# The fourth token sum of a seven-product FFN, issued in pieces among the first chain's products

## The chip, the cores and the metric

The kernel runs on one core of one Trainium2 chip. The metric is the device time of one execution in microseconds (us). The core has TensorE (PE in the profile; PEld is its loading of weights), VectorE (DVE), ScalarE (ACT), GpSimd (POOL) and SyncE (SP); the last two issue most of the DMAs here.

## What is computed

Two layers of a decoder on 512 tokens of width 1024. The first layer mixes tokens with dilated attention, the second with a recurrent block, and each is followed by a gated convolutional FFN, which is what the change touches:

```python
def conv_ffn(x, w_up, conv_w, conv_b, w_down):
    u = causal_dwconv(x @ w_up, conv_w, conv_b)      # (512, 6144), three taps along the tokens
    g, v = u[..., :D_FF], u[..., D_FF:]              # D_FF = 3072
    return (jax.nn.gelu(g, approximate=True) * v) @ w_down
```

All data are float32. Norms stand before and after each part.

## The kernel before, in words

**Precision.** A float32 operand is split (`split`, L148) into a rounded half `hi` (ScalarE, L149) and the residue `lo` (VectorE, L150). A product is three passes, hi x hi, hi x lo and lo x hi. Weights come as blocks of 1 MB by SyncE (`load`, L331), at most three at a time, and are split on the way.

**The up projection.** Its output is made in tiles of 128 features by 512 tokens; twelve groups j of 256 features for g and twelve for v. Groups 0 to 2 are made plainly (`feat_tile`, L623: one weight, all tokens, 24 matmuls of 512 columns). Groups 3 to 11 (`SEVEN`, L39) are made by a scheme of Strassen's kind (`seven`, L1047): a 256 x 512 x 1024 product is cut into two by two blocks and made from seven block products instead of eight, at the price of sums. Nine groups times two halves (g, v) are the 18 chains. A chain (L1010) has seven products of twelve matmuls of 256 columns, numbered 1 to 7. Their left operands are blocks of a raw weight or sums of them, made in place: s1, w11, w12, s2, s3, s4, a22. VectorE makes some of these sums (L210, L214), and GpSimd the others, as DMAs that add (L186). Their right operands are blocks of the activations hT, or one of four sums T of them, made once per FFN by `token_sums` (L918).

**Slots.** `seven` gives every product a slot number m (`AT`, L41): in a chain that starts at 10 n, product 1 stands at 10 n, 5 at +1, 2 at +2, 6 at +4, 3 at +5, 7 at +8, 4 at +13. So the products of the first chain stand at m = 0, 1, 2, 4, 5, 8 and 13, those of the second from m = 10 on. Free slots (m = 9, 16, 17, 19 and so on) take quarters of a plain tile or early parts of the down projection. Numbers with nothing in them are passed over. In each slot (`slot`, L365) the product is issued first, then what earlier slots put off (`later`, L362), then a `tick` (L377). What is put off are copies of part results (`part`, ScalarE, L1032), sums of part results (L1036, L1041), and the tile's end: eviction with the first tap (ScalarE, L773), two more taps (VectorE, L777), gelu (ScalarE, L795) or gate (VectorE, L799). Product 6 accumulates into the bank of product 1, so it has to wait for the copy of product 1's result; product 3 likewise for product 5's.

**Ticks.** A tick advances the generators in `sides` (each yields the number of ticks to its next step), then calls `pump` (L303) unless `state["hold"]` is set:

```python
        if not state["hold"]:
            pump(1 if state["even"] or state["live"] >= HALVES - 4 else 2)
```

`pump` takes the next piece of weight from a fixed order (`stream`, L199), splits it into one of 16 pairs of buffers, issues the sums that stand behind it in the order, and loads the next raw block when the last piece of an old one is taken. `live` counts the buffers in use; a product frees its own (`done`, L354). While `seven` runs, `state["even"]` is set: one piece per tick. If a product's piece has not been split when the product is issued, `take` (L347) pumps it then.

**The token sums.** `token_sums` runs as such a generator beside the plain tiles. With first=False (the FFN) it starts at the FFN's fifth tick and takes one tick per step: keep x and take buffers; add the two halves of hT's blocks back together (L939); T0 = b11 - b12 and its split; b22; two more differences (L964, L945); the split of T1; the split of T2; then, at the twelfth tick, b21 and its two differences (L945); at the thirteenth the split of the last sum, T3 (two tiles, homes 6 and 7). `seven` starts after the fourteenth. T3 is the right operand of product 4, which the first chain has at m = 13. Attention calls the same function with first=True and two ticks to a step.

The engines take their instructions in the order of issue, each from its own queue, so the order in which slots and ticks issue them sets what stands in front of what.

Of the kernel before, what the change touches and what calls it, by code (L numbers as in the profile page):

```python
# [32 lines left out]
HALVES = 16  # L33
# [8 lines left out]
CYCLE = 10  # L42
# [41 lines left out]
def kernel(  # L84
# [38 lines left out]
    def nm(s):  # L123
        uid[0] += 1
        return f"{s}{uid[0]}"

    def gen(dt=F32, s="g"):
        return gp.tile([P, 512], dt, tag="g", name=nm(s))

    def psum(s="ps"):  # L130
        return pp.tile([P, 512], F32, tag="ps", name=nm(s))
# [16 lines left out]
    def split(hi, lo, raw):  # L148
        nc.scalar.activation(hi, raw, AF.Copy)  # L149
        nc.vector.tensor_tensor(lo, raw, hi.bitcast(F32), op=ALU.subtract)  # L150

    plan = []
    state = {"dma": 0, "cv": 0, "used": 0, "live": 0, "next": 0, "hold": False, "even": False, "quiet": False}
# [124 lines left out]
    def refill():  # L278

        i = state["cv"]  # L280
        if i >= state["dma"]:
            return
        if plan[i][0] == "quad":
            pieces.extend(strided_stream(i))
            state["cv"] += 24
            return
        if plan[i][0] == "seven":
            n = 1
            while plan[i + n][0] == "seven":
                n += 1  # L290
            pieces.extend(stream(i, n))
            state["cv"] += n
        else:
            if plan[i + 1 : i + 2] and plan[i + 1][0] == "seven":
                pieces.append((None, lambda: ahead(i + 1)))
            parts = parts_of(plan[i][0], raws[i])
            pieces.extend(plain(i, j, r, j == len(parts) - 1) for j, r in enumerate(parts))
            state["cv"] += 1

    def single(name):  # L300
        return (name[0] if isinstance(name, tuple) else name) in HALF

    def pump(limit=2):  # L303

        for _ in range(limit):
            if not pieces:
                refill()
            while pieces and pieces[0][0] is None:
                pieces.pop(0)[1]()
            if not pieces or pieces[0][0][0] >= state["dma"]:  # L310
                continue
            if state["live"] + 2 - single(pieces[0][0][1]) <= HALVES:
                key, cuts, last = pieces.pop(0)
                cuts = cuts()
                his, los = [], []
                for n, raw in enumerate(cuts):
                    hi, lo = (
                        wp.tile([P] + list(raw.shape[1:]), F32R, tag=t, name=nm("w" + t)) for t in ("hi", "lo")
                    )
                    split(hi, lo, raw)  # L320
                    his.append(hi)
                    los.append(lo)
                units[key] = (his, los)
                state["live"] += len(cuts)
                state["used"] += last
                while pieces and pieces[0][0] is None:
                    pieces.pop(0)[1]()
            while not state["quiet"] and state["dma"] < len(plan) and state["dma"] - state["used"] < RAW_BUFS:
                load()

    def load():  # L331
        i = state["dma"]
        kind, kd, cols, srcs = plan[i][:4]
        raw = wp.tile([P, kd, cols], F32, tag="raw", name=nm("raw"), bufs=RAW_BUFS)
        at = 0
        for src, n in srcs:
            nc.sync.dma_start(raw[:, :, at : at + n] if kind == "value" else raw[:, at : at + n, :], src)
            at += n
        raws[i] = raw
        state["dma"] += 1  # L340
# [21 lines left out]
    def later(n, f):  # L362
        due.append([n, f])

    def slot(emit, length=1):  # L365
        emit()
        for d in list(due):
            d[0] -= 1
            if d[0] < 0:
                due.remove(d)  # L370
                d[1]()
        tick(length)
# [545 lines left out]
    def token_sums(hT, T, first=False):  # L918

        if not first:  # L920
            assert len(sides) == 1, len(sides)
            d = dp.tile([P, 4, D], F32, name=nm("x_kept"))
            nc.gpsimd.dma_start(d, X[0])
            kept.append(d)
        homes = cp.tile([P, 4, D], F32R, tag="x_sb", name=nm("T"))
        homes = [homes[:, n] for n in range(4)]
        homes += [cp.tile([P, D], F32R, tag="gain", name=nm("T"), bufs=2) for _ in range(1 if first else 2)]
        homes = [[h[:, 0:512], h[:, 512:1024]] for h in homes]
        if first:
            homes += [[gen(F32R, "T") for _ in range(2)]]  # L930
        homes += [[wp.tile([P, 512], F32R, tag=t, name=nm("T")) for _ in range(2)] for t in ("hi", "lo")]
        state["live"] += 2
        homes = [[h.rearrange("p (k t) -> p k t", k=2) for h in hs] for hs in homes]
        yield 1 + first

        def both(k0, n):
            o = gen(s="B").rearrange("p (k t) -> p k t", k=2)
            hi, lo = (h[:, k0 : k0 + 2, n * 256 : n * 256 + 256] for h in hT)
            tt(o, hi.bitcast(F32), lo.bitcast(F32), op=ALU.add)  # L939
            return o  # L940

        tt = nc.vector.tensor_tensor

        def negative(o, a, b):
            nc.vector.scalar_tensor_tensor(o, a, -1.0, b, op0=ALU.mult, op1=ALU.subtract)  # L945

        def whole(k0, n):
            return [both(k0 + 2 * k, n) for k in range(2)]

        def parted(n, b):  # L950
            for k in range(2):
                split(homes[2 * n][k], homes[2 * n + 1][k], b[k])

        b11, b12 = whole(0, 0), whole(0, 1)
        yield 1 + first
        for k in range(2):
            tt(b11[k], b11[k], b12[k], op=ALU.subtract)
        parted(0, b11)
        yield 1 + first
        b22 = whole(4, 1)  # L960
        if not first:
            yield 1
        for k in range(2):
            tt(b12[k], b22[k], b12[k], op=ALU.subtract)  # L964
            negative(b22[k], b11[k], b22[k])
        yield 1 + first
        parted(1, b22)
        T.extend([homes[2 * n], homes[2 * n + 1]] for n in range(4))
        yield 1 + first
        parted(2, b12)  # L970
        yield 1 + first
        b21 = whole(4, 0)
        if first:
            yield 2
        for k in range(2):
            negative(b21[k], b22[k], b21[k])
        yield 1 + first
        parted(3, b21)

    LEFT = {5: ("s1", 1), 1: ("w11", 0), 3: ("s4", 1), 2: ("w12", 0), 6: ("s2", 1), 7: ("s3", 1), 4: ("a22", 1)}  # L980

# [65 lines left out]
    def seven(hT, T, begin, last, prep):  # L1047

        right = rights(hT, T)
        i0, acc, ends_at = state["next"], {}, CYCLE * 2 * len(SEVEN)  # L1050

        def finish(b, ps, j, minus=False):
            later(2, begin(b, ps, j, minus, True))

        def ends(j, half):
            return (
                lambda ps: later(0, lambda: finish(2 * half, ps, j)),
                lambda ps: finish(2 * half + 1, ps, j, True),
            )

        def rows(k, pair):
            W, A = take(i0, ("rows", k)), take(i0, ("act", k))
            for t in pair:
                if t not in acc:
                    acc[t] = psum("acc")
                mm3(acc[t], [a[0][:, t * P : (t + 1) * P] for a in A], [w[0] for w in W], not k, False)
            if pair[-1] == 3:
                done(2)

        fill = []  # L1070
        for m in range(2):
            fill += quarters(last, m, hT, lambda ps, m=m: finish(2 + m, ps, SEVEN[0] - 1))
        fill += [lambda k=k, p=p: rows(k, p) for k in range(REST[0]) for p in ((0, 1), (2, 3))]
        steps = {}
        n = 0
        for j in SEVEN:
            for half in range(2):
                f = chain(right, *ends(j, half))
                steps.update((CYCLE * n + AT[p], f(p)) for p in AT)
                n += 1  # L1080
        free = free_slots(n)
        assert len(free) == len(fill)
        steps.update(zip(free, fill))
        state["even"] = True
        for m in range(max(steps) + 1):
            if m == ends_at - 2:
                prep()
            if m in steps:
                slot(steps[m])
        while due:  # L1090
            slot(lambda: None)
        done(2)
        state["even"] = False
        return acc
# [626 lines left out]
```

## Time and profile before

| | us |
|---|---|
| median of three runs | 1421.13 (1419.31 to 1421.55) |
| the profiled execution | 1420.89 |
| its span, first to last instruction | 1419.1 |
| TensorE busy in it | 1406.0 |
| VectorE busy | 1125.1 |
| ScalarE busy | 800.6 |

The page is of one profiled execution. Busy time counts instructions on an engine; matmuls are pipelined, so a busy TensorE need not be at its peak. A timeline's row is start, length, engine, line, operation, output <- input, shape and count; in brackets stands the idle time ahead of it and what ended it. Names are those of the program: `raw` a weight as loaded, `whi` and `wlo` its halves, `T` a token sum, `B` a part of one, `ps` a bank of results, `part` a copy of one, `u` a tile behind the up projection.

### The profile page before, as it was taken

The page shows a single profiled execution, that of the slowest core. Times are in us where ns is not written, and L with a number is a line of the kernel's source. Part 1 is how long each engine was busy: PE and PEld are TensorE (multiplying, and loading weights), DVE is VectorE, ACT ScalarE, POOL GpSimd, SP SyncE. Part 2 cuts the span into 40 slices and gives each one's busy share as a digit, 9 for nine tenths or more (in the row PEclk, how much of TensorE's full clock was granted, in tenths as well). Part 3 has the DMA queues.
Part 4 walks back from the last instruction along what each step waited for, and adds up shares of the span by engine and source line. Part 5 has one row for each costly group of instructions (what it writes and reads, how often), then busy time and mean ns, then how long its engine had stood idle before and what let it go on. Part 6 is the DMA issues. An engine that isn't in the chain of part 4 may idle for free.

```text
span 1419.1 us, 23634 instructions
## 1 busy us (share of the span) xinstructions
PE 1406.0 (99%) x8741; PEld 1267.6 (89%) x8741; DVE 1125.1 (79%) x2201; ACT 800.6 (56%) x1646; POOL 225.8 (16%) x344
## 2 busy tenths in 40 slices
PE   9999999999999999999999999999999999999998
PEld 7888999999998898999999888888898999999886
DVE  6676898887866988998888758769789898888843
ACT  7343565353636555666666645589455666666641
POOL 0441332131300102221110001000101212111000
PEclk9999999999999999999999999999999999999999
DMA  7643464655655445666663632431435757665411
GB/s 227 181 145 110 122 178 150 174 162 162 177 184 186 160 149 115 152 153 159 128 151 89 212 129 90 134 119 63 145 127 113 171 118 164 153 130 127 165 58 60
DMA packets 171886, 201.93 MB, mean 142 GB/s; under 512 B 10561, under 2 KB 141081, under 8 KB 171513
## 3 DMA queue, kind: packets, MB, share of 16 engines
q1 hardware_dynamic: 123064, 153.34, 33.8%
q0 software_dynamic: 47856, 46.02, 17.6%
q8 instruction: 69, 1.13, 0.3%
q10 hardware_dynamic: 848, 1.05, 0.2%
q14 instruction: 49, 0.39, 0.1%
HBM read 181.41 MB, written 18.96 MB: 141 GB/s over the span
## 4 chain that ended last, share of the span: by engine, by line
PE 83%; DVE 9%; ACT 5%; issue 1%; DMA 0%; POOL 0%; DVEq 0%; ACTq 0%
PE ps L1023 35%; PE acc L412 25%; PE ps L412 11%; PE v L1219 7%; DVE wlo L150 3%; DVE u L777 2%; PE v L1157 1%; DVE xb L1524 1%; PE O L1431 1%; PE S L1365 1%; ACT whi L149 1%; PE S L1313 1%; DVE T L150 1%; DVE B L939 1%; ACT sig L1545 1%
## 5 line engine op out<-in xcount | busy, mean ns | idle before, releaser
L150 DVE TENSOR_TENSOR wlo<-raw,whi 128x512 fp32r<-128x512 f32 x620 | 410.7, 686 | 112.1 <-ACT whi L149 109.5
L149 ACT ACTIVATE whi<-raw 128x512 fp32r<-128x512 f32 x620 | 371.0, 626 | 189.3 <-PE ps L1023 76.3
L1023 PE MATMUL ps<-T,whi 128*128 128x256 f32 x1664 | 304.3, 283 | 4.2 <-ACT part L1032 3.5
L412 PE MATMUL ps<-hT,whi 128*128 128x512 f32 (+1 forms) x1088 | 288.0, 353 | 0.0
L1023 PEld LDWEIGHTS ps<-T,whi 128*128 128x128 f32 x1664 | 259.3, 190 | 8.9 <-ACT part L1032 3.9
L1023 PE MATMUL ps<-T,wlo 128*128 128x256 f32 x832 | 233.3, 280 | 0.0
L1023 PE MATMUL ps<-hT,whi 128*128 128x256 f32 x1248 | 231.4, 284 | 0.0
L412 PEld LDWEIGHTS ps<-hT,whi 128*128 128x128 f32 x1088 | 190.8, 189 | 26.4
L1023 PEld LDWEIGHTS ps<-hT,whi 128*128 128x128 f32 x1248 | 196.6, 192 | 2.6
L412 PE MATMUL ps<-hT,wlo 128*128 128x512 f32 (+1 forms) x544 | 191.3, 352 | 0.0
L1023 PE MATMUL ps<-hT,wlo 128*128 128x256 f32 x624 | 176.8, 283 | 0.0
L186 POOL DMA_DIRECT2D raw<-in_ffn_w_up_dram x72 | 92.8, 1318 | 424.4 <-DVE wlo L150 291.2
L1023 PEld LDWEIGHTS ps<-T,wlo 128*128 128x128 f32 x832 | 158.4, 190 | 0.0
L412 PE MATMUL acc<-whi,ahi 128*128 128x512 f32 x352 | 137.7, 391 | 0.0
L412 PE MATMUL acc<-whi,alo 128*128 128x512 f32 x352 | 137.2, 390 | 0.2
L412 PE MATMUL acc<-wlo,ahi 128*128 128x512 f32 x352 | 137.0, 389 | 0.0
L1023 PEld LDWEIGHTS ps<-hT,wlo 128*128 128x128 f32 x624 | 119.8, 192 | 0.0
L412 PEld LDWEIGHTS ps<-hT,wlo 128*128 128x128 f32 x544 | 102.9, 189 | 14.0
L1219 PE MATMUL v<-whi,hT 128*128 128x512 f32 x320 | 106.5, 396 | 0.0
L1032 ACT ACTIVATE part<-ps 128x256 f32<-128x256 f32 x156 | 58.7, 376 | 71.7 <-PE ps L1023 68.7
L777 DVE SCALAR_TENSOR_TENSOR u<-ps,cols,u 128x511 f32<-128x511 f32 x120 | 89.4, 746 | 5.0 <-ACT u L773 2.9
L412 PEld LDWEIGHTS acc<-whi,alo 128*128 128x128 f32 x352 | 66.1, 188 | 14.9 <-DVE alo L150 1.1
(206 smaller groups left out, 2125.5 us busy)
## 6 DMA issues: line engine op xcount, KB each, us to landing
raw<-in_ffn_w_up_dram SPq DMA_DIRECT2D x48, 1024.0 KB
raw<-in_attn_w_qkv_dram SPq DMA_DIRECT2D x67, 512.0 KB
raw<-in_ffn_w_up_dram POOLq DMA_DIRECT2D x72, 256.0 KB, 4.9
raw<-in_ffn_w_down_dram SPq DMA_DIRECT2D x14, 1024.0 KB
dw<-in_ffn_w_down_dram SPq DMA_DIRECT2D x40, 256.0 KB
raw<-in_lru_w_in_dram SPq DMA_DIRECT2D x8, 1024.0 KB
turned<-T POOLq DMA_DIRECT2D x26, 256.0 KB, 2.6
ft<-turned POOLq DMA_DIRECT2D x104, 64.0 KB, 4.6
```

What stands on the lines that cost most here:

```text
L149: nc.scalar.activation(hi, raw, AF.Copy)
L150: nc.vector.tensor_tensor(lo, raw, hi.bitcast(F32), op=ALU.subtract)
L186: nc.gpsimd.dma_start(to, src, accum_op=ALU.add)
L412: mm(dst, l[a], r[b], start=start and n == 0, stop=stop and n == 2)
L777: nc.vector.scalar_tensor_tensor(u[:, d:], ps[:, : S - d], wc, u[:, d:], op0=ALU.mult, op1=ALU.add)
L939: tt(o, hi.bitcast(F32), lo.bitcast(F32), op=ALU.add)
L1023: mm(dst, W[wa][0][:, k, :], right[n](ha, k), start=n in (1, 5) and k == q == 0, stop=k == 3 and q == 2, skip_group_check=True,)
L1032: later(1, lambda: nc.scalar.activation(to, dst, AF.Copy))
L1157: mm(banks[t], hT[a][:, k, t * P : (t + 1) * P], W[b][k % 2][:, 0, :], start=u == n == 0, stop=u == 3 and n == 5,)
L1219: mm(bank, hT[a][:, k, t * P : (t + 1) * P], W[b][k % 2][:, 0, :], start=(k, a, b) == (0, 0, 0), stop=(k, a, b) == (KD - 1, 1, 0),)
L1313: mm(Sp[a // 2][:, o + lo : o + 256], q[hh][:, a * P : (a + 1) * P], k[hh][:, k0 : (a + 1) * P], start=True, stop=True)
L1365: mm(ps[:, c], q[hh][:, c], k[hh][:, c], start=True, stop=True)
```

## The change

In the FFN the two differences that make b21 into the fourth sum, and the two splits of that sum, leave the twelfth and thirteenth tick. After b21 the generator waits three ticks, and so goes on in the tick of m = 0. There it issues the first difference and holds the pump, so that this tick takes no piece of weight; in the tick of m = 1 it lets the pump go again; at m = 2 comes the second difference, at m = 5 the first split and at m = 9 the second, each with the pump held, and at m = 4, 8 and 10 the pump is let go. At slots with m over 20 and divisible by 5, one more piece is pumped after the tick, if fewer than 14 buffers are live then. With first=True the order of attention is kept by cases of its own.

```diff
@@ token_sums
         b21 = whole(4, 0)
+        yield 2 if first else 3
+        for k in range(2):
+            if not first:
+                state["hold"] = True
+            negative(b21[k], b22[k], b21[k])
+            if not first:
+                yield 1
+                state["hold"] = False
+                yield 1
         if first:
             yield 2
+            parted(3, b21)
+            return
         for k in range(2):
-            negative(b21[k], b22[k], b21[k])
-        yield 1 + first
-        parted(3, b21)
+            state["hold"] = True
+            split(homes[6][k], homes[7][k], b21[k])
+            yield 1
+            state["hold"] = False
+            yield 1
@@ seven
             if m in steps:
                 slot(steps[m])
+                if m > 2 * CYCLE and m % 5 == 0 and state["live"] < HALVES - 2:
+                    pump(1)
```

## The prediction

> **What bounds the kernel now.** I read the page first, its span and its busy line; then the list of what TensorE waited for (us in total, times, longest).
>
> ```profile
> span 1419.1 us, 23634 instructions
> ...
> PE 1406.0 (99%) x8741; PEld 1267.6 (89%) x8741; DVE 1125.1 (79%) x2201; ACT 800.6 (56%) x1646; POOL 225.8 (16%) x344
> ```
>
> ```profile
> PE ps L1023 <- ACT part L1032: 3.5, 2, 1.8
> PE warm L1640 <- DVE one L1685: 1.5, 1, 1.5
> PE ps L1023 <- DVE ps L1041: 0.7, 1, 0.7
> ```
>
> TensorE is busy for 99% of the span, so a change on the other engines can give back only the few waits that are left. The largest is for one copy on ScalarE (L1032), twice, 1.8 us each. The timeline of TensorE shows where, once in each FFN; the chain in order of time (start, length, what) gives the pace around it.
>
> ```profile
> 540.70 0.61 PE L412 MATMUL ps<-hT,whi 128*128 128x512 f32 x2
> ...
> 548.99 0.40 PE L1023 MATMUL ps<-hT,whi 128*128 128x256 f32 x2
> ...
> 552.36 0.50 PE L1023 MATMUL ps<-T,whi 128*128 128x256 f32 x2 [1.77 <-ACT part L1032]
> ...
> 1090.67 0.40 PE L1023 MATMUL ps<-hT,whi 128*128 128x256 f32 x2
> ...
> 1094.03 0.50 PE L1023 MATMUL ps<-T,whi 128*128 128x256 f32 x2 [1.77 <-ACT part L1032]
> ```
>
> ```profile
> 552.36 6.05 PE ps L1023 x36
> ...
> 1094.03 4.53 PE ps L1023 x36
> 1099.94 8.58 PE ps L1023 x72
> ```
>
> A chain's product is twelve matmuls: 8.58 x 12 / 72 = 1.43 us. Slot m=2 of the first chain starts at 548.99 (so m=0 at 548.99 - 2.86 = 546.13). Slot m=4, the next that holds a product, should follow at 548.99 + 1.43 = 550.42 and comes at 552.36: **1.94 us lost**. In the second FFN it is 1094.03 - 1090.67 - 1.43 = 1.93 us. Behind the first gap the same 36 matmuls take 6.05 us, behind the second 4.53: **1.52 us more**. The table by stretches (busy time of PE, PEld, DVE, ACT, POOL, then granted clock, DMA share, GB/s) says why:
>
> ```profile
> 552.00:575.00 23.00, 22.64 (x155) 21.64 (x156) 18.70 (x29) 15.19 (x30) 5.11 (x4) 0.93 0.78 168
> 575.00:600.00 25.00, 25.00 (x184) 23.75 (x184) 22.86 (x38) 15.30 (x29) 5.16 (x4) 1.00 0.67 148
> ...
> 1094.00:1117.00 23.00, 22.97 (x170) 21.96 (x171) 20.01 (x33) 15.82 (x30) 5.12 (x4) 1.00 0.86 177
> ```
>
> The granted clock is 0.93 right behind the first gap, 1.00 behind the second. I charge the 1.52 us to the first gap, with a rival below.
>
> Why is the copy late? VectorE's timeline, then ScalarE's:
>
> ```profile
> 541.80 1.28 DVE L945 SCALAR_TENSOR_TENSOR B<-B,B 128x512 f32<-128x512 f32 x2
> 543.01 0.68 DVE L150 TENSOR_TENSOR wlo<-raw,whi 128x512 fp32r<-128x512 f32 x1
> 543.61 0.68 DVE L210 TENSOR_TENSOR raw<-raw 128x512 f32<-128x512 f32 x1
> 544.21 0.68 DVE L799 TENSOR_TENSOR u<-u,u 128x512 f32<-128x512 f32 x1
> 544.82 1.52 DVE L777 SCALAR_TENSOR_TENSOR u<-ps,cols,u 128x511 f32<-128x511 f32 x2
> 546.26 1.28 DVE L150 TENSOR_TENSOR T<-B,T 128x512 fp32r<-128x512 f32 x2
> 547.46 1.29 DVE L150 TENSOR_TENSOR wlo<-raw,whi 128x512 fp32r<-128x512 f32 x2
> 548.66 0.69 DVE L214 TENSOR_TENSOR raw<-raw 128x512 f32<-128x512 f32 x1
> 549.26 1.53 DVE L777 SCALAR_TENSOR_TENSOR u<-ps,cols,u 128x511 f32<-128x511 f32 x2
> ```
>
> ```profile
> 540.90 0.78 ACT L773 ACTIVATE u<-ps,cols 128x512 f32<-128x512 f32 x1 [3.17 <-PE ps L412]
> ...
> 550.88 0.63 ACT L795 ACTIVATE u<-u 128x512 f32<-128x512 f32 x1 [0.87 <-DVE u L777]
> 551.42 0.61 ACT L149 ACTIVATE whi<-raw 128x512 fp32r<-128x512 f32 x1
> 551.94 0.36 ACT L1032 ACTIVATE part<-ps 128x256 f32<-128x256 f32 x1
> ```
>
> No row of VectorE has an idle time in brackets: it is behind. The last plain tile's taps (L777) start at 549.26; ScalarE's gelu (L795) waits for them until 550.88; behind it in ScalarE's queue stand one weight piece's rounding and only then the copy. So VectorE's backlog, by way of ScalarE's queue, stops TensorE.
>
> **The change, part by part.** *Taken from in front of the copy.* Two differences (L945, 541.80) and two residues (L150 into T, 546.26) leave VectorE's queue there. Two of a kind take 1.20 us to the next start (546.26 to 547.46), one 0.60, the four 2.40 us. Two roundings leave ScalarE's queue, where they ran while it waited for VectorE anyway. And the tick of m=0 is held, so the rounding at 551.42 no longer stands ahead of the copy: 0.52 us (551.94 - 551.42).
>
> *When the copy runs then.* The taps could start at 549.26 - 2.40 = 546.86, but read the last plain tile after its eviction. The eviction of the tile before started 0.20 us after its product (540.90; the next product began at 540.70) and took 0.78. The last product ends where m=0 begins, 546.13: eviction over at 546.13 + 0.20 + 0.78 = 547.11. Taps 547.15 to 548.68; gelu from 548.77; copy 0.54 later (551.42 - 550.88), 549.31 to 549.67. TensorE wants m=4 at 550.42. **The wait goes, with 0.75 us to spare**: 1.94 + 1.93 = 3.87 us, and with the gap the 1.52 us that I charged to it.
>
> *Put into the first chain's slots.* Difference at m=0, difference at m=2, split at m=5, split at m=9; these four ticks take no weight piece. For VectorE that is four instructions in and four pieces' residues put off; but the stream of pieces runs four behind. By the code, one piece leaves per tick, in a fixed order. The next seven are the second chain's s1 and w12, the first's a22, the third's w11, the second's s2, s3 and s4: before at m=0, 1, 2, 4, 5, 8, 9; now at m=1, 4, 8, 10, 11, 12, 13. The second chain reads s2 at m=14 and s4 at m=15. So s4 has two slots of lead instead of six, s2 three instead of seven; every other piece of the 18 chains keeps five or more.
>
> *What is late next*, then, is s4 at m=15. TensorE has nine slots from m=4 to m=14: 550.42 + 9 x 1.43 = 563.3. VectorE, free at 548.7, does six instructions of 0.60 (two residues left over, difference, residue, difference, residue) to 552.3. ScalarE copies m=4's product after 551.9 and rounds the first half of T; residue over at 553.5. Then the top sum (m=5 over at 553.3), residue of a22, L210, lower sum, second residue of T, two taps, two residues, L214: ten instructions at 0.60 to 0.75, near 559.6. The second half of T, the last part of the fourth sum, is done by 556.5 and read at m=13 (560.4). ScalarE gets to s3 and s4 after the copy of m=11's product (over at 559.0) and a gelu, at 559.9 to 561.0; the residue of s4 ends near 561.8. That is an estimate, summed from the durations quoted: 1.5 us ahead of 563.3, so these edits cost nothing as long as that cover holds. Were it gone, the nearest rows are TensorE's wait of 0.7 us (L1041) and that of 1.94 us; a gain beyond the waits named is excluded, since TensorE has none there. I take 0, the end to which the sum is nearest, and keep 0.7 and 1.94 per FFN for the range.
>
> *DMA and queues.* No transfer is added. The load into the first chain's raw block waits on SyncE for the residue of a22, now issued at m=8 instead of m=2; but VectorE was late then, and by the count above the residue ends at 554.8.
>
> ```profile
> 554.37 0.37 SPq L337 DMA_DIRECT2D raw<-in_ffn_w_up_dram  x1
> ```
>
> The load went out at 554.37: 0.4 us apart. GpSimd's adds into the raw blocks are released by residues and loads, not by slots, and the pieces' order between an add and its reader stays. The ones that the first sums of the chains wait for (534 to 538 us) landed as follows (least, median, most), so the first is in by 541.5, ahead of L210 even where that moves up to 542.4.
>
> ```profile
> DMA to landing us min/median/max: 4.8/5.3/5.8
> ```
>
> *The extra pump* (m over 20, divisible by 5, fewer than 14 halves live): counted through, it fires once per FFN, at m=25 (11 live); from m=30 on the tick leaves 14. The stream then runs one piece behind until m=171, where the old one found no room and the new one draws level. No instruction more: nothing.
>
> *Attention* (first=True) issues the same list in the same ticks: nothing.
>
> **Sum**, against the profiled execution's 1420.89 us (1.79 of it around the span): 1420.89 - 3.87 - 1.52 = **1415.50 us**. The median shown is 1421.13, of runs from 1419.31 to 1421.55. The lowest is near 1420.89 - 1.52 = 1419.37, as if it had no dip of the clock; from there 3.87 less is 1415.5 again.
>
> The Trainium skill, "TensorE: Matmul & The Clock Gate", section "What's actually happening", halves the clock after at least one idle window of about 3.4 us, in windows that run free. By that length a gap of 1.77 us would never do it, the dip would have another cause, and the sum would be 1420.89 - 3.87 = 1417.0; the trace has the dip behind one of two such gaps, which speaks for the free-running windows and against the strict length.
>
> **The rivals.**
> 1. *A new wait takes the old one's place*, at s4 or s2 of the second chain. For it: two and three slots of lead. Against: 1.5 us of cover. Were VectorE 3.1 us later than I count, TensorE would wait 1.6 us in each FFN: 1415.5 + 3.2 = 1418.7.
> 2. *The dip stays*, because something other than the gap makes it: 1420.89 - 3.87 = 1417.0. For it: the second gap has none. Against: the clock is 1.00 in the neighbouring stretches.
> 3. *The change doesn't do what it says*: something besides these instructions holds the copy (an add that VectorE must wait for once its backlog is gone), and half of the wait stays, the dip too: 1420.89 - 1.94 = 1418.95.
> 4. *Slower*: the stream one piece behind, in a stage where VectorE is busy for 22.86 of 25 us. If L210, in VectorE's queue, reached its add before that landed, all behind it would stand, and each later chain would lose time: 16 chains in each of two FFNs at 0.27 us are 8.6: 1424.1. It decides once a sum comes up on its add by more than VectorE's idle time of a chain (2.14 of 25 us, 1.2 for ten slots). The unchanged order of pieces speaks against it.
>
> **How the numbers follow.** Forecast 57%, rival 1 14%, rival 2 17%, rival 3 8%, rival 4 4%. Predicted: 1415.5. The range starts 0.9 below, half the distance of the lowest run from the median (1421.13 - 1419.31), and reaches to 1418.7, past rival 2, rival 1 and the bound of 0.7 per FFN; it leaves out rivals 3 and 4 and some of rival 1, 15 in 100. A measurement of this kernel can tell about 0.2%, 2.8 us: faster is under 1418.3. The forecast, rival 2 and two thirds of rival 1 (smaller waits) lie there: 0.83. The rest of rival 1 and rival 3 are the same: 0.13. Slower: 0.04.
>
> **What would show it.** Right: no wait of L1023 for L1032; slot m=4 some 4.3 us after m=0 in both FFNs; the first copy over by about 549.7; a clock of 1.00 in the stretch behind; T's last residues between m=5 and m=10; the load near 554.8. Wrong: a wait of L1023 for L150 at m=14 or 15; a dip without a gap; VectorE idle ahead of L210.

## The result and the profile after

The changed kernel takes 1415.55 us (median of six, 1415.16 to 1416.66), the kernel before 1421.17 in the same rounds: a ratio of 0.9964, 95% interval 0.9951 to 0.9976. That is 5.6 us less; 1415.5 was predicted. The profiled execution took 1415.33 us.

The span on the page after, and the list of what TensorE waited for (us in total, times, longest). In the code after, L1036 is the old L1023 (a chain's product), L1045 the old L1032 (the copy), L1049 and L1054 the old L1036 and L1041 (the sums of part results).

```profile
span 1413.6 us, 23534 instructions
```

```profile
PE warm L1655 <- DVE one L1700: 1.5, 1, 1.5
PE ps L1036 <- DVE ps L1054: 0.7, 1, 0.7
PE v L1172 <- ACT whi L149: 0.3, 1, 0.3
PE tr L513 <- DMA x_sb<-in_x_dram: 0.3, 1, 0.3
PE v L1172 <- DVE wlo L150: 0.2, 1, 0.2
```

The wait for the copy is gone from the list; the two of 0.3 us lie in the first 7 us of the kernel. TensorE's timeline at the first chain of each FFN, and the stretches behind them with the granted clock (the third figure from the end):

```profile
546.24 0.40 PE L1036 MATMUL ps<-hT,whi 128*128 128x256 f32 x2
...
550.52 0.40 PE L1036 MATMUL ps<-T,whi 128*128 128x256 f32 x2
...
1084.29 0.40 PE L1036 MATMUL ps<-hT,whi 128*128 128x256 f32 x2
```

```profile
552.00:575.00 23.00, 23.00 (x173) 22.00 (x173) 19.70 (x33) 14.18 (x27) 5.11 (x4) 1.00 0.64 150
...
1072.00:1094.00 22.00, 22.00 (x132) 19.65 (x132) 20.95 (x35) 13.55 (x25) 5.20 (x4) 1.00 0.52 92
1094.00:1117.00 23.00, 23.00 (x177) 22.20 (x176) 20.32 (x33) 14.82 (x29) 5.12 (x4) 1.00 0.73 162
```

Slot m=4 starts 4.28 us after m=0, three products of 1.43 with nothing between, and the clock is 1.00 behind it. The time can be laid out by three marks: the first chain of the first FFN (546.14 before, 546.24 after), that of the second (1087.82 and 1084.29), and the end of the span. The two marks of the kernel before:

```profile
546.14 0.40 PE L1023 MATMUL ps<-hT,whi 128*128 128x256 f32 x2
...
1087.82 0.40 PE L1023 MATMUL ps<-hT,whi 128*128 128x256 f32 x2
```

From first to second it is 541.68 us before and 538.05 after, 3.63 less, where 1.94 + 1.52 were predicted; from the second to the end 331.28 and 329.31, 1.97 less, where 1.93 were. Ahead of the first, 0.10 more.

ScalarE's queue after, then VectorE's:

```profile
546.44 0.78 ACT L773 ACTIVATE u<-ps,cols 128x512 f32<-128x512 f32 x1 [0.49 <-PE ps L412]
...
548.88 0.63 ACT L795 ACTIVATE u<-u 128x512 f32<-128x512 f32 x1 [0.62 <-DVE u L777]
549.41 0.37 ACT L1045 ACTIVATE part<-ps 128x256 f32<-128x256 f32 x1
...
560.66 0.38 ACT L1045 ACTIVATE part<-ps 128x256 f32<-128x256 f32 x1 [1.43 <-PE ps L1036]
560.94 1.14 ACT L149 ACTIVATE whi<-raw 128x512 fp32r<-128x512 f32 x2
```

```profile
547.25 1.53 DVE L777 SCALAR_TENSOR_TENSOR u<-ps,cols,u 128x511 f32<-128x511 f32 x2 [0.22 <-ACT u L773]
548.70 1.28 DVE L150 TENSOR_TENSOR wlo<-raw,whi 128x512 fp32r<-128x512 f32 x2
549.90 0.68 DVE L945 SCALAR_TENSOR_TENSOR B<-B,B 128x512 f32<-128x512 f32 x1
...
553.08 0.69 DVE L150 TENSOR_TENSOR T<-B,T 128x512 fp32r<-128x512 f32 x1 [0.69 <-ACT T L149]
...
561.60 1.29 DVE L150 TENSOR_TENSOR wlo<-raw,whi 128x512 fp32r<-128x512 f32 x2 [1.56 <-ACT whi L149]
```

The taps (547.25) now wait 0.22 us for their eviction instead of being late themselves; the gelu and the copy follow at once; the differences and residues of the fourth sum stand behind. The load behind the first chain went out at 555.00, 0.2 us from the forecast:

```profile
555.00 0.37 SPq L337 DMA_DIRECT2D raw<-in_ffn_w_up_dram  x1
```

### The profile page after: what moved, and what is told of

Its sections match the earlier page's. It is cut to its first block, busy times and chain, and to the rows that moved or that the text cites. A ratio compares the mean times of both kernels' runs of the same rounds, so it can differ in the third digit from the quotient of the medians.

```text
span 1413.6 us, 23534 instructions
## 1 busy us (share of the span) xinstructions
PE 1403.6 (99%) x8741; PEld 1266.1 (90%) x8741; DVE 1122.2 (79%) x2201; ACT 792.4 (56%) x1646; POOL 224.9 (16%) x344
## 4 chain that ended last, share of the span: by engine, by line
PE 90%; DVE 4%; ACT 4%; issue 1%; DMA 0%; POOL 0%; DVEq 0%; ACTq 0%
PE ps L1036 36%; PE acc L412 25%; PE ps L412 17%; PE v L1234 7%; PE v L1172 1%; DVE wlo L150 1%; DVE xb L1539 1%; PE O L1446 1%; PE S L1380 1%; PE S L1328 1%; ACT whi L149 1%; ACT sig L1560 1%; PE tr L502 1%; PE O L412 0%; ACT sig L1579 0%
## 5 line engine op out<-in xcount | busy, mean ns | idle before, releaser
L150 DVE TENSOR_TENSOR wlo<-raw,whi 128x512 fp32r<-128x512 f32 x620 | 408.4, 685 | 119.0 <-ACT whi L149 117.1
L149 ACT ACTIVATE whi<-raw 128x512 fp32r<-128x512 f32 x620 | 367.0, 625 | 151.8 <-PE acc L412 48.0
L1036 PE MATMUL ps<-T,whi 128*128 128x256 f32 x1664 | 303.6, 283 | 0.7 <-DVE ps L1054 0.7
L1036 PEld LDWEIGHTS ps<-T,whi 128*128 128x128 f32 x1664 | 259.0, 190 | 5.0 <-DVE ps L1054 1.1
L1036 PE MATMUL ps<-T,wlo 128*128 128x256 f32 x832 | 233.2, 280 | 0.0
L1036 PE MATMUL ps<-hT,whi 128*128 128x256 f32 x1248 | 230.5, 283 | 0.0
L1036 PEld LDWEIGHTS ps<-hT,whi 128*128 128x128 f32 x1248 | 195.8, 191 | 2.6
L1036 PE MATMUL ps<-hT,wlo 128*128 128x256 f32 x624 | 176.7, 283 | 0.0
L1036 PEld LDWEIGHTS ps<-T,wlo 128*128 128x128 f32 x832 | 158.4, 190 | 0.0
L1036 PEld LDWEIGHTS ps<-hT,wlo 128*128 128x128 f32 x624 | 119.5, 191 | 0.0
L1045 ACT ACTIVATE part<-ps 128x256 f32<-128x256 f32 x156 | 59.0, 378 | 97.2 <-PE ps L1036 93.9
L773 ACT ACTIVATE u<-ps,cols 128x512 f32<-128x512 f32 x60 | 46.2, 774 | 63.0 <-DVE ps L1049 48.9
```

What stands on the lines that cost most here:

```text
L773: nc.scalar.activation(u, ps, AF.Identity, scale=own[:, j : j + 1], bias=cc[:, 48 + j : 49 + j])
L1036: mm(dst, W[wa][0][:, k, :], right[n](ha, k), start=n in (1, 5) and k == q == 0, stop=k == 3 and q == 2, skip_group_check=True,)
L1045: later(1, lambda: nc.scalar.activation(to, dst, AF.Copy))
```

## The experiments

The theory is the prediction's: VectorE's backlog, by way of the gelu in ScalarE's queue, held one copy, and the gap this made in TensorE's work cost a dip of the clock besides. Each edit is against the kernel named. Gaps are computed as the start of m=4 less the start of m=0 less 4.29 us (three products).

**Only the held ticks, nothing moved** (before):

```diff
             if m in steps:
+                state["hold"] = m in (0, 2, 5, 9)
                 slot(steps[m])
```

> The kernel before with the ticks of m=0, 2, 5 and 9 held, the token sum where it was. Theory: only the one rounding leaves the queue ahead of the copy, 0.52 us: the gap shrinks from 1.94 to about 1.4 us in each FFN, 1419.9 with a dip of the clock, 1418.4 without. Rival (the held pump is what helps): no gap, 1415.5.

Measured: 1419.98 us, ratio 0.9995 (0.9986 to 1.0004). TensorE's timeline:

```profile
546.43 0.40 PE L1023 MATMUL ps<-hT,whi 128*128 128x256 f32 x2
...
552.12 0.50 PE L1023 MATMUL ps<-T,whi 128*128 128x256 f32 x2 [1.25 <-ACT part L1032]
...
1086.43 0.40 PE L1023 MATMUL ps<-hT,whi 128*128 128x256 f32 x2
...
1092.41 0.50 PE L1023 MATMUL ps<-T,whi 128*128 128x256 f32 x2 [1.53 <-ACT part L1032]
```

The first gap is 552.12 - 546.43 - 4.29 = 1.40 us (1.94 - 0.52 = 1.42 by the queue). The second is 1.69 us: there the taps ahead of the gelu start 3.40 us after m=0, where they started 3.12 us after it in the kernel before. Holding the pump alone is not the gain. The time is not as expected: the profile has no dip, so 1418.4 was due, and the profiled execution took 1419.69. The marks say where most of it went. Less its gaps, this kernel takes 1086.43 - 546.43 - 1.40 = 538.60 us and 1417.9 - 1086.43 - 1.69 = 329.78 us; the kernel before, less its gaps and its dip, takes 538.22 and 329.35. So the held ticks cost 0.4 us in each FFN, which the theory had at nothing.

**Moved, but no tick held** (after): the two lines `state["hold"] = True` taken out.

```diff
-            if not first:
-                state["hold"] = True
             negative(b21[k], b22[k], b21[k])
...
-            state["hold"] = True
             split(homes[6][k], homes[7][k], b21[k])
```

> The changed kernel with the differences and splits in the slots, but every tick takes its weight piece again. Theory (VectorE's backlog, by way of the gelu in ScalarE's queue, held the copy): one weight rounding of 0.52 us is back in front of the copy, which starts at 549.9 instead of 549.4 and ends at 550.3, still 0.2 us before TensorE wants it: no gap, 1415.5 to 1416.0. Rival (the held pump is what helps): the gap of 1.9 us is back in both FFNs, 1419.5 to 1421.

Measured: 1415.36 us, ratio 0.9965 (0.9955 to 0.9975). ScalarE's timeline:

```profile
549.27 0.62 ACT L149 ACTIVATE whi<-raw 128x512 fp32r<-128x512 f32 x1
549.79 0.36 ACT L1042 ACTIVATE part<-ps 128x256 f32<-128x256 f32 x1
```

The rounding stands before the copy again, the copy ends at 550.15, 0.2 us before TensorE asks for it, and there is no gap. So the move makes the gain and the holds add nothing that can be measured. Two of the nine executions took 1418.40 and 1418.98 us, at a granted clock of 0.998; no profile shows what happened in them.

**Only the splits moved** (before), the differences left in the twelfth tick, m=5 and m=9 held:

```diff
         for k in range(2):
             negative(b21[k], b22[k], b21[k])
-        yield 1 + first
-        parted(3, b21)
+        yield 2 if first else 7
+        if first:
+            parted(3, b21)
+            return
+        for k in range(2):
+            state["hold"] = True
+            split(homes[6][k], homes[7][k], b21[k])
+            yield 1
+            state["hold"] = False
+            yield 1
```

> The kernel before with only the two splits of the fourth sum moved to m=5 and m=9 (those two ticks held); the differences stay in the twelfth tick, and m=0 pumps as before. Theory: two residues, 1.20 us, leave VectorE's queue ahead of the copy: the gap shrinks from 1.94 to about 0.74 us in each FFN, 1420.9 - 2.4 = 1418.5, or 1417.0 where the clock does not dip. Rival (all or nothing, one cause besides the queue): 1421 or 1415.5.

Measured: 1417.3 us, ratio 0.9977 (0.9968 to 0.9985).

```profile
546.30 0.40 PE L1031 MATMUL ps<-hT,whi 128*128 128x256 f32 x2
...
551.32 0.51 PE L1031 MATMUL ps<-T,whi 128*128 128x256 f32 x2 [0.57 <-ACT part L1040]
```

The gap is 0.73 us against 0.74 by 1.94 - 1.20: the gap goes down by just what leaves VectorE's queue, in the second FFN too. There is no dip, and 1417.0 was expected without one.

**Nothing moved but the gelu** (before):

```diff
-        tiles(SEVEN[0] - 1, chunk(), (0, 1))
+        i, j = chunk(), SEVEN[0] - 1
+        feat_tile(i, 0, hT, lambda ps: begin(0, ps, j))
+        feat_tile(i, 1, hT, lambda ps: later(2, begin(1, ps, j)))
```

> The kernel before with one thing moved: the gelu of the last plain tile is issued two slots later, behind the copy of product 1. VectorE's backlog stays. Theory (the backlog reaches TensorE only by the gelu in ScalarE's queue): the copy follows the roundings at about 550.4 and ends at 550.8, a gap of about 0.4 us is left in each FFN, 1416.4. Rival (the copy or product 6 waits for VectorE directly): the gap stays at 1.9 us, 1420 to 1421.

Measured: 1416.31 us, ratio 0.9970 (0.9958 to 0.9981).

```profile
546.32 0.40 PE L1025 MATMUL ps<-hT,whi 128*128 128x256 f32 x2
...
551.05 0.50 PE L1025 MATMUL ps<-T,whi 128*128 128x256 f32 x2 [0.28 <-ACT part L1034]
```

The gap is 0.44 us, with VectorE's backlog as it was. This is the sharpest test: not the backlog itself but one ScalarE instruction that waited for it, ahead of the copy in the queue, stopped TensorE. Three lines bring 4.8 us against the kernel before in the same rounds (1421.08), where the whole change brings 5.6.

**The copy made late** (after), with needless copies in front of it (three, then five; the diff shows the five):

```diff
+        def late(n):
+            t = gen(s="late")
+            for _ in range(n):
+                nc.scalar.activation(t, hT[0][:, 0, :].bitcast(F32), AF.Copy)
...
             if m in steps:
+                if not m:
+                    later(1, lambda: late(5))
                 slot(steps[m])
```

> The changed kernel with three needless ScalarE copies of 128x512 in front of the first chain's copy. Theory: the copy starts 3 x 0.52 = 1.56 us later, spends its 0.7 us of cover and holds TensorE for about 0.9 us in each FFN, with no dip of the clock: 1417.3. Rival (TensorE does not wait for this copy alone): 1415.5.

Measured: 1418.12 us, ratio 0.9985 (0.9976 to 0.9994).

```profile
546.23 0.40 PE L1036 MATMUL ps<-hT,whi 128*128 128x256 f32 x2
...
551.68 0.51 PE L1036 MATMUL ps<-T,whi 128*128 128x256 f32 x2 [1.00 <-ACT part L1045]
```

A gap of 1.16 us, not 0.9: the three copies, which write one tile, took 1.94 us, where I had taken 0.52 each. The two gaps make 0.5 of the 0.8 us by which the time is over the forecast. No dip.

> The same with five needless copies: the gap of the kernel before, about 1.9 us in each FFN, without its order. Theory (a gap of this length makes the clock dip when it falls well into a window): 1419.4 without a dip, 1420.9 with one, so 1419.4 to 1421 in different executions, and granted clocks below 1.00 behind some gaps. Rival (the dip has another cause): 1419.4 in all of them, the clock at 1.00 behind both gaps.

Measured: 1423.1 us (1422.2 to 1425.5), ratio 1.0018 (1.0010 to 1.0027), slower than before. TensorE's timeline, the chain, and the stretch behind the second gap, which was at full clock before:

```profile
546.18 0.40 PE L1036 MATMUL ps<-hT,whi 128*128 128x256 f32 x2
...
552.95 0.51 PE L1036 MATMUL ps<-T,whi 128*128 128x256 f32 x2 [2.32 <-ACT part L1045]
```

```profile
552.95 6.04 PE ps L1036 x36
...
1095.09 6.04 PE ps L1036 x36
```

```profile
1094.00:1117.00 23.00, 21.91 (x149) 20.91 (x150) 17.15 (x28) 14.42 (x29) 3.84 (x3) 0.93 0.47 113
```

The gap is 2.48 us, longer than meant, for the same reason, and the time is above the range that was expected; two such gaps and two dips of 1.5 us over 1415.5 make 1423.5, and the profiled execution took 1423.48. The clock dips behind both gaps, 6.04 us for 36 matmuls as behind the one dip of the kernel before (6.05, against 4.53 without). The order of the changed kernel with a gap put in dips as the old one did: **the gap makes the dip**. The needless copies by themselves don't: three of them, with 1.00 us of idling, made none.

**A fifth held tick**, at m=12 (after):

```diff
             if m in steps:
+                if m in (12, 13):
+                    state["hold"] = m == 12
                 slot(steps[m])
```

> The changed kernel with a fifth held tick, at m=12: block s4 of the second chain is split at m=14 and read at m=15. Theory: the lead of the four holds is close to the least that serves (0.4 to 0.7 us of cover in the changed kernel's own timeline); with the fifth, s4's residue ends near 564.1 and product 3 at m=15, from 563.4 on, waits about 0.7 us in each FFN: 1417.0. Rival (the cover is 1.5 us as in the prediction): no wait, 1415.5.

Measured: 1417.34 us, ratio 0.9973 (0.9963 to 0.9984). TensorE's timeline at m=15:

```profile
564.61 0.38 PE L1036 MATMUL ps<-hT,wlo 128*128 128x256 f32 x1 [0.22 <-DVE wlo L150]
```

The loading of the weights for the same product has a wait for the rounding ahead of it:

```profile
563.88 0.30 PEld L1036 LDWEIGHTS ps<-hT,whi 128*128 128x128 f32 x2 [0.18 <-ACT whi L149]
```

The second chain's s4 is late, at the product where rival 1 put the wait, and TensorE's list has the wait for its residue twice, once in each FFN, 0.22 us each. In all the first chains of the two FFNs start 538.78 us apart (546.66 to 1085.44) against 538.05 in the changed kernel: 0.73 us for the fifth hold, as expected.

**No extra pump** (after):

```diff
-                if m > 2 * CYCLE and m % 5 == 0 and state["live"] < HALVES - 2:
-                    pump(1)
```

> The changed kernel without the extra pump at m=25. Theory (the wait for the copy was all): the extra pump only evens the stream out, no wait of L1036 for a weight residue appears, and the time stays at 1415.5 within 0.5. Rival (the stream one to four pieces behind would starve the later chains without it): waits of the chains' products for L150 from the third chain on, 1417 or more.

Measured: 1416.82 us, ratio 0.9972 (0.9963 to 0.9981): neither theory's number. One of the eleven executions took 1420.09 us, at a granted clock of 0.997, and wasn't profiled. No wait for L150 is there, but a small one for a sum, at about the same place in each FFN:

```profile
602.56 0.50 PE L1036 MATMUL ps<-T,whi 128*128 128x256 f32 x2 [0.15 <-DVE ps L1054]
```

So I ran it once more beside the changed kernel itself.

> The changed kernel, unaltered, on the same chip and in the same rounds as the next kernel. Theory: no gap behind the first chains, no dip of the clock in any execution: 1415.2 to 1416.6 as before, median 1415.5. Rival (dips come without gaps too): some executions 1.5 us above the rest.

> The changed kernel without the extra pump, once more, beside the changed kernel itself. Its first profile had two new waits for L1054, 0.2 us each, with the whole FFN 0.4 us longer, and 0.8 us more in attention, whose instructions are the same. Theory: only the FFN's part belongs to the edit: 0.8 us over the changed kernel in the same rounds, and attention's wait for L1054 lies anywhere from 0.6 to 1.5 us in either kernel. Rival: attention's part comes with this build too, 1.3 to 1.7 us over it every time.

Measured in the same rounds: 1415.88 us with the pump, ratio 0.9961 (0.9948 to 0.9973), and 1416.67 without, ratio 0.9967 (0.9956 to 0.9979). The first chains' starts, with the pump and without:

```profile
546.77 0.40 PE L1036 MATMUL ps<-hT,whi 128*128 128x256 f32 x2
...
1084.78 0.40 PE L1036 MATMUL ps<-hT,whi 128*128 128x256 f32 x2
```

```profile
548.96 0.40 PE L1036 MATMUL ps<-hT,whi 128*128 128x256 f32 x2
...
1087.37 0.40 PE L1036 MATMUL ps<-hT,whi 128*128 128x256 f32 x2
```

From the first FFN to the second it is 538.01 us with the pump and 538.41 without, and from there to the end (spans of 1414.0 and 1417.0 us) 329.22 and 329.63: **0.4 us per FFN** is the missing piece's, 0.8 in all, as the medians say. None of the five executions with the pump, 1415.44 to 1416.90 us, has a clock below 0.999, so no dip shows without a gap. The rest of what the profiled execution without the pump took, 1418.82 us, lies in attention, whose instructions are the same. It doesn't come every time: five of the seven executions took 1416.18 to 1417.08 us. VectorE and TensorE in attention, then the stretch:

```profile
202.32 0.69 DVE L246 TENSOR_TENSOR raw<-raw 128x512 f32<-128x512 f32 x1 [1.00 <-DMA raw<-in_attn_w_qkv_dram]
```

```profile
211.54 0.50 PE L1036 MATMUL ps<-T,whi 128*128 128x256 f32 x2 [1.75 <-DVE ps L1054]
```

```profile
209.00:215.00 6.00, 4.25 (x20) 3.46 (x19) 5.05 (x10) 1.86 (x3) 0.00 (x0) 0.81 0.00 0
```

A load of weights landed 1.0 us late for a sum on VectorE, everything behind it stood, TensorE idled 1.75 us, more than the 1.5 that was expected at most, and the clock fell. In the changed kernel's first profile VectorE doesn't wait for that load, and TensorE idles 0.7 us at full clock. All twelve profiles fit: in the six without that wait of VectorE TensorE idles there for 0.6 to 0.7 us, and waits of 0.21, 0.30, 0.56, 0.63, 0.76 and 1.00 go with 0.95, 1.03, 1.28, 1.36, 1.49 and 1.75 us.

## Why the prediction was right, step by step

- *What holds TensorE*: right, and shown from both sides. Moving the gelu behind the copy takes the gap to 0.44 us; delaying the copy brings it back.
- *What leaves the queue*: right. Forecast for the copy 549.31 to 549.67, measured 549.41 to 549.78; the gap fell by what was taken out (1.20 by two residues in both FFNs; 0.52 by the hold in the first, while in the second the taps themselves came 0.28 us later).
- *The dip belongs to the gap*: right. By the idle time that the rows show, it came behind 1.75, 1.77 and 2.32 us (twice), not behind the other gap of 1.77 of the kernel before, nor behind 1.53, 1.49, 1.25, 1.00, 0.57 and 0.28. The 30 executions of the kernel before beside the second four experiments lie in steps of 1.5 us: nine at 1419.31 to 1419.82, seven at 1420.77 to 1420.87, the rest above or between. Each one's mean granted clock is on record and goes the same way: 0.999 up to 1420.30 us, 0.997 or 0.998 from 1420.77 to 1421.72, and 0.996 from 1422.88; the profiles have 0.998 with one dip and 0.996 with two. That the steps are none, one and two dips is the likely reading. It isn't shown, since two profiles without a dip also have 0.998. Rival 2, that the dip has another cause than a gap, is out for the profiled executions; the four slow ones of kernels without this gap that weren't profiled (two without holds, two without the extra pump) may have had attention's gap; that stays open.
- *Why one of two equal gaps dips*: the prediction leaned on windows that run free, and the traces bear it out. In all twelve, every change of the granted clock stands a whole number of steps of 3.413 us behind the start of the trace's record of the clock, and between the start and the end of a kernel the half clock lasts one step. The steps around the two gaps of the kernel before (stretch, length, TensorE's busy time first; the clock third from the end):

```profile
549.79:553.20 3.41, 1.64 (x14) 1.44 (x13) 3.20 (x6) 2.54 (x7) 1.24 (x1) 1.00 0.96 119
553.20:556.61 3.41, 3.41 (x19) 3.41 (x18) 3.22 (x6) 2.41 (x5) 0.77 (x1) 0.50 0.56 113
1089.10:1092.51 3.41, 3.17 (x27) 2.96 (x25) 3.38 (x7) 1.46 (x3) 1.76 (x2) 1.00 0.00 0
1092.51:1095.92 3.41, 1.89 (x16) 1.89 (x17) 3.14 (x5) 3.36 (x8) 0.82 (x1) 1.00 1.14 140
```

The first gap lies in one step, idle for 3.41 - 1.64 = 1.77 us, and the next step has half the clock. The second is cut by an edge, 0.24 and 1.52 us, and no step is halved. The other dips in mid-kernel follow steps with 1.75, 2.32 and 2.18 us of idling; no step with 1.53 or less is followed by one. So the dip goes with where a gap falls on these steps, and they lie differently in each execution: in the twelve traces the first begins 4.7 to 8.1 us behind the kernel's first instruction. It isn't the whole rule: at the kernel's end, steps with 1.81 (first profile after) and 1.90 us (fifth hold) weren't followed by a halved one.
- *The rule weighed*: the Trainium skill, "TensorE: Matmul & The Clock Gate", "What's actually happening", asks for an idle window of about 3.4 us. The traces have the clock halved for 3.41 us at a time, which agrees, but behind 1.75 to 2.32 us of idling, which doesn't. A gap need not fill a window.
- *What is late next*: the place was right, the cover mis-sized. I gave s4's residue 1.5 us; it ends at 562.89 (561.60 + 1.29), and m=15 starts at 563.32: 0.4 us. I let ScalarE copy m=11's product when that ended, 559.0. In the trace the copy starts at 560.66, at the end of m=12, which writes the other half of the same bank. The roundings of s3 and s4 stand behind it. With one hold more the wait is there. Rival 1's wait was nearer than the 1.5 us of cover said.
- *The extra pump at nothing*: wrong by itself. Without it each FFN has a wait of 0.15 us shown and 0.4 in all: the four held ticks cost that much, as they also do with nothing moved, and the extra piece pays it back. The prediction put both at nothing. The two together come to nothing, so here the sum was right by two small errors that cancel, which is luck.
- *Rival 3* (half the wait stays) and *rival 4* (the stream starves): neither in any FFN. The mechanism of rival 4, a sum at the head of VectorE's queue waiting for its transfer, does occur in attention: the load that was 1.0 us late in the second run without the extra pump, and less late in five other profiles.

No version ran that beats the changed kernel beyond the measurement; the one without holds (1415.36 us) equals it with less code.

## What to carry to other kernels

When a saturated engine has one gap, follow the releaser back through the queues: the instruction to move may be on a third engine, and here one gelu put behind one copy was worth most of moving four instructions. Before paying for a fix with held work, try it without holding, and count the lead of each piece put off by what its engine must finish first (a copy may wait for a neighbour in the same bank), not by slots. A gap of under 2 us on TensorE can cost its length and 1.5 us more by the clock, and whether it does can differ from one execution to the next.

## What the runs showed of the hardware

Not expected: the clock halves for 3.41 us behind 1.75 us of idling, and not behind every 1.77; its changes stand on a grid of 3.413 us, and in mid-kernel a step with 1.75 us or more of idling was followed by a halved one, one with 1.53 or less wasn't. Three ScalarE copies of 128x512 into one tile take 1.94 us (0.62 from one start to the next, as the copy behind them started 1.85 us after the first), where roundings into different tiles start 0.52 us apart; whether the tile makes the difference no run shows. TensorE's wait for the sum in attention (L1054 in the changed kernel) lies between 0.6 and 1.8 us in the twelve profiles, whose instructions there are the same; a late load of weights goes with each wait of 0.9 us and more. What makes the load late wasn't tried.
